# Feed-forward down projection over both streams as seven products, weight sums on GpSimd, in a two-layer encoder trunk

## The chip, the cores and the metric

One core of a Trainium2 chip runs the whole program. The metric is device time in microseconds (us), the median of three runs. The engines are TensorE (PE, with its weight loads PEld), VectorE (DVE), ScalarE (ACT), GpSimd (POOL) and SyncE (SP, which issues the loads).

## What is computed

Two streams of 512 tokens, width 1024, go through two layers with shared weights, and a final norm. The part at issue is the gated feed-forward of each layer, here from the reference:

```
h = _rmsnorm(x, norm_ffn)
gate, up = jnp.split(h @ ffn_w_up, 2, axis=-1)
gate = _dwconv3(gate, ffn_conv)
x = x + (jax.nn.gelu(gate) * up) @ ffn_w_down
```

`ffn_w_up` is 1024 x 5632 and `ffn_w_down` 2816 x 1024. Ahead of it stands a mixer (retention heads, a long convolution, pooling) with input and output projections, behind it a gate by a per-layer embedding.

## The kernel before

Activations lie transposed: 128 channels on the partitions, 512 tokens of one stream along the free axis. A width of 1024 is eight such tiles, the inner width of 2816 is 22.

**Three matmuls for one.** Each float32 operand is split into two float16 parts (`split`, L173): ACT writes the high part, DVE the rest. A product of two tiles is then three float16 matmuls of 128x128 by 512 columns: high by high, high by low, low by high.

**Weights.** SP loads raw float32 tiles (128x1024, `wraw`, four buffers) in the order of the list `TILES`; ACT and DVE split them into `wspl` tiles (nine buffers). The functions `plan_weights` and `prep` (L186, L217) cut this into pieces and issue them ahead of use, up to 21 us by a table of estimated step times (`step_time`, L115) and as far as the nine buffers allow.

**Up projection.** The first three of 22 pairs of a gate tile and an up tile are made for each stream by itself (`f.hn`, `fg`, `fu`). For the other 19 the two streams are taken together: the weight's two columns (gate, up), its two halves of K, and the two streams form a 2x2 by 2x2 product that needs seven products instead of eight (Strassen in Winograd's form). Such a pair is called a *unit* here. It needs sums of activations (`ffn_sums`, L1010, once per layer) and four sums of weights per unit (`piece_pair`, L273, on DVE before), which overwrite the raw tiles. The seven products run in three PSUM banks X, Y, Z, in the order X, Y, Z, X, Y, X, X (`ffn_joint`, L1038; `product`, L1096): the later ones accumulate onto what lies there, so each bank must be read between two of them. The results are read as `r1`, `r5`, `r2` (ACT copies) and by sums on DVE; then come the convolution (`conv3`, L556), the gelu, and `gated` (L1003), which multiplies by the up half and splits the result into an `at` tile for the down projection.

**Down projection.** The 22 `at` tiles of a stream are used in four parts (`PARTS`, L31): 6, 6, 5 and 5 of them. After the last unit of a part come its eight output tiles (`d0_0` to `d0_7` and so on), each for stream 0 and then stream 1 (`down`, L1034, with `mm3`, L302): for part 0 that is 6 x 3 matmuls each, and DVE adds the bank onto the residual tile `x`. The last part belongs to the streams' own threads (`main_thread`, L828).

**Order.** The list `STEPS` (`tile_order`, L87) fixes the order of these steps on PE. Within a layer it puts the first products of the next unit between the last two of a unit:

```
            last = steps.pop(cut)
            steps[cut:cut] = [seven[0], last, seven[1], seven[2]]
            steps += seven[3:]
```

So PE's order in the middle of the stage is: product 5 of unit j, product 0 of unit j+1, product 6 of unit j, products 1, 2, 3, 4, 5 of unit j+1. PE and SP keep the written order; DVE, ACT and POOL are put in order at build time by the tile framework, each then runs its queue strictly in that order.

## Time and profile before

| | |
|---|---|
| median of 3 runs | 2510.44 us (2508.78 to 2511.34) |
| the profiled execution: its time, its span | 2508.9 us, 2507.1 us |
| busy: PE, PEld | 2431.4 us (97%), 1191.8 us (48%), 12240 matmuls and as many loads |
| busy: DVE, ACT, POOL | 1639.4 us (65%), 985.7 us (39%), 368.3 us (15%) |
| stage of the joint units and down parts 0 to 2 | about 622 to 1141 us (layer 0), 1808 to 2327 us (layer 1) |

Busy times of PE overlap from one matmul to the next, since their ends are modelled; the start-to-start time is what a matmul costs. The same holds for DVE, more weakly: an instruction shown as 0.69 us is followed by the next one after 0.60 us. Rows of the trace name the line of the helper that records an instruction (L155 `act`, L158 `stt`, L161 `tt`), so they are told apart by their tiles.

### The profile page before, as it was taken

What the parts mean: (1) busy time and instruction counts of PE and PEld (TensorE: products, weight loads), DVE (VectorE), ACT (ScalarE), POOL (GpSimd) and SP (SyncE); (2) the same over time, 40 slices, a digit from 0 to 9 for tenths busy, and PEclk for the clock granted to TensorE, in tenths of its full rate; (3) what the DMA queues carried; (4) which work ended last, traced back from release to release, by engine and by line L of the source; (5) the groups of instructions that cost most, each with busy time, mean ns of one, the idle gap of its engine ahead of it and who ended that gap; (6) DMA issues with size and microseconds to landing.
All of it is one profiled execution on the core that took longest, in us unless ns stands there. A gap on an engine that the chain in (4) does not pass through costs nothing.

```text
span 2507.1 us, 30755 instructions
## 1 busy us (share of the span) xinstructions
PE 2431.4 (97%) x12240; PEld 1191.8 (48%) x12240; DVE 1639.4 (65%) x2530; ACT 985.7 (39%) x1567; POOL 368.3 (15%) x294
## 2 busy tenths in 40 slices
PE   5999989999999999999999999999999999999997
PEld 3544654444444444444456555544444444444443
DVE  6984886868737557475575686555964755757545
ACT  5543334345515325243533343333541532524441
POOL 3213343123000000000121223511300000000011
PEclk9999999999999999999999999999999999999998
DMA  6122020340201201112232111031021120212201
GB/s 221 64 82 75 25 69 18 116 133 34 82 34 62 73 34 59 51 68 87 69 121 89 65 48 52 28 112 64 34 68 34 64 72 34 68 43 76 84 1 67
DMA packets 63927, 168.05 MB, mean 67 GB/s; under 512 B 7526, under 2 KB 13670, under 8 KB 63784
## 3 DMA queue, kind: packets, MB, share of 16 engines
q1 hardware_dynamic: 57880, 155.87, 18.4%
q10 hardware_dynamic: 5904, 10.23, 1.1%
q8 instruction: 95, 1.56, 0.3%
q14 instruction: 48, 0.39, 0.1%
HBM read 151.65 MB, written 14.42 MB: 66 GB/s over the span
## 4 chain that ended last, share of the span: by engine, by line
PE 75%; DVE 4%; POOL 1%; issue 1%; ACT 1%; ACTq 0%; POOLq 0%; DVEq 0%
PE fx L1100 16%; PE fy L1100 8%; PE d L311 6%; PE d L309 6%; PE d L310 6%; PE fz L1100 4%; PE s L309 2%; PE s L311 2%; PE s L310 2%; PE o L310 2%; PE o L311 2%; PE o L309 2%; PE fu L309 1%; PE fu L311 1%; PE fu L310 1%
## 5 line engine op out<-in xcount | busy, mean ns | idle before, releaser
L155 ACT ACTIVATE wspl<-wraw 128x512 f16<-128x512 f32 (+3 forms) x426 | 309.9, 744 | 483.3 <-PE d L311 273.8
L1100 PEld LDWEIGHTS <-wspl 128*128 128x128 f16 x3192 | 312.3, 98 | 379.2 <-issue 2.8
L158 DVE SCALAR_TENSOR_TENSOR wspl<-wraw,wspl 128x512 f16<-128x512 f32 (+3 forms) x420 | 346.1, 837 | 110.9 <-ACT wspl L155 109.0
L309 PEld LDWEIGHTS <-wspl 128*128 128x128 f16 x2112 | 208.9, 99 | 250.4 <-issue 8.9
L311 PEld LDWEIGHTS <-wspl 128*128 128x128 f16 x2112 | 207.2, 98 | 252.4 <-issue 4.7
L310 PEld LDWEIGHTS <-wspl 128*128 128x128 f16 x2112 | 207.2, 98 | 252.2 <-issue 11.6
L1100 PE MATMUL fx<-hs,wspl 128*128 128x512 f16 x1368 | 313.9, 379 | 2.2 <-DVE r L161 2.2
L309 PE MATMUL d<-at,wspl 128*128 128x512 f16 x704 | 266.8, 379 | 0.0
L310 PE MATMUL d<-at,wspl 128*128 128x512 f16 x704 | 266.8, 379 | 0.0
L311 PE MATMUL d<-at,wspl 128*128 128x512 f16 x704 | 266.8, 379 | 0.0
L158 DVE SCALAR_TENSOR_TENSOR x<-d,x 128x512 f32<-128x512 f32 x128 | 88.5, 691 | 254.2 <-PE d L311 253.9
L161 POOL TENSOR_TENSOR y<-t,mhalf 128x4 f32<-128x4 f32 x30 | 36.3, 1211 | 1416.5 <-DVE t L165 1407.2
L158 DVE SCALAR_TENSOR_TENSOR conv<-r,scaled,conv 128x511 f32<-128x511 f32 x152 | 113.7, 748 | 44.3 <-ACT conv L155 42.6
L161 DVE TENSOR_TENSOR wraw<-wraw 128x512 f32<-128x512 f32 x152 | 104.3, 686 | 1.9
L1100 PE MATMUL fx<-h,wspl 128*128 128x512 f16 x456 | 104.6, 379 | 0.0
L1100 PE MATMUL fy<-h,wspl 128*128 128x512 f16 x456 | 104.6, 379 | 0.0
L1100 PE MATMUL fy<-hs,wspl 128*128 128x512 f16 x456 | 104.6, 379 | 0.0
L1100 PE MATMUL fz<-h,wspl 128*128 128x512 f16 x456 | 104.6, 379 | 0.0
L161 DVE TENSOR_TENSOR acc<-acc,sq 128x512 f32<-128x512 f32 x84 | 64.0, 766 | 51.0 <-ACT sq L155 49.7
L155 ACT ACTIVATE sq<-x 128x512 f32<-128x512 f32 x80 | 49.6, 624 | 121.4 <-DVE x L158 53.3
L311 PE MATMUL s<-xs,wspl 128*128 128x512 f16 x256 | 97.0, 379 | 0.0
L310 PE MATMUL s<-xs,wspl 128*128 128x512 f16 x256 | 97.0, 379 | 0.0
(236 smaller groups left out, 4417.9 us busy)
## 6 DMA issues: line engine op xcount, KB each, us to landing
wraw<-in_w SPq DMA_DIRECT2D x172, 512.0 KB, 3.5
wraw<-in_w SPq DMA_DIRECT2D x32, 384.0 KB, 3.3
wraw<-in_w SPq DMA_DIRECT2D x32, 320.0 KB, 3.0
x<-in_x SPq DMA_DIRECT2D x32, 256.0 KB, 4.1
dec<-ddec SPq DMA_DIRECT2D x16, 448.0 KB, 4.0
xsp<-x ACTq DMA_DIRECT2D x16, 256.0 KB, 2.1
x<-xsp SPq DMA_DIRECT2D x16, 256.0 KB, 3.8
out_y<-out SPq DMA_DIRECT2D x16, 256.0 KB, 2.2
```

The costliest lines, as they stand in the source:

```text
L155: return self.nc.scalar.activation(out=out, in_=in_, func=func, **k)
L158: return self.nc.vector.scalar_tensor_tensor(out=out, in0=in0, scalar=scalar, in1=in1, op0=op0, op1=op1)
L161: return (eng or self.nc.vector).tensor_tensor(out=out, in0=in0, in1=in1, op=op)
L309: self.nc.tensor.matmul(out, wv[:, 0, kb, :], x[:, 0], start=first, stop=False)
L310: self.nc.tensor.matmul(out, wv[:, 0, kb, :], x[:, 1], start=False, stop=False)
L311: self.nc.tensor.matmul(out, wv[:, 1, kb, :], x[:, 0], start=False, stop=last)
L1100: mm = lambda a, b, start=False, stop=False: self.nc.tensor.matmul(out, a, b, start=start, stop=stop, skip_group_check=not first)
```

## The change

- `PARTS` becomes 6, 6, 6 and 4 tiles, and the first three parts (`JOINT = 3`) are done for both streams together: two output tiles, the two members of each pair of `at` tiles, and the two streams form the 2x2 by 2x2 product, with seven products of 3 x 3 matmuls per pair of output tiles. The steps are `e{part}_{pair}.{0..6}`, in banks X, Y, Z as before, and DVE adds each of the seven results onto a residual tile.
- `gated` no longer only splits: for each pair of `at` tiles it makes four sums of activations on DVE and splits seven tiles instead of four.
- The weight tiles of two outputs are regrouped on the host (`pack`) into `ea`, `eb`, and go through `piece_pair` as the gate and up tiles do.
- In `piece_pair` the four weight sums move from DVE to POOL, and the seven splits of 512 columns become four: 1024, 512, 1024, 1024 (768, 384, 768, 768 for the down weights).
- The pool of general tiles grows from 64 to 70, and the scratch area for dynamic DMAs is set to 2048.

```diff
-PARTS = [(0, 6), (6, 12), (12, 17), (17, 22)]
+PARTS = [(0, 6), (6, 12), (12, 18), (18, 22)]
+JOINT = 3
...
-            if j == b - 1:
+            if j == b - 1 and t < JOINT:
+                tiles += [f"e{x}{t}_{i}" for i in range(NB // 2) for x in "ab"]
+
+                for i in range(NB // 2 + 1):
+                    now, old = ([f"e{t}_{k}.{q}" for q in range(7)] for k in (i, i - 1))
+                    if i == 0:
+                        steps += now[:5]
+                    elif i < NB // 2:
+                        steps += [now[0], old[5], now[1], now[2], old[6], now[3], now[4]]
+                    else:
+                        steps += old[5:]
+            elif j == b - 1:
...
-        self.gp = pool("gen", 64)
+        self.gp = pool("gen", 70)
...
-                    self.pieces += [(self.piece_pair, l, j, k) for k in range(7)]
-                wants.append((self.piece_pair, l, j, (0, 2, 3, 4, 5, 6, 6)[int(q)]))
+                    self.pieces += [(self.piece_pair, l, j, k) for k in range(4)]
+                wants.append((self.piece_pair, l, j, (0, 2, 2, 3, 3, 3, 3)[int(q)]))
...
     def piece_pair(self, l, j, k):
 
-        g, u = (self.rawt[l, n + j[1:]] for n in ("fg", "fu"))
-        a11, a12, a21, a22 = g[:, 0:512], g[:, 512:1024], u[:, 0:512], u[:, 512:1024]
-        if k in (0, 1, 3, 5):
-            self.wt[l, j, k] = self.wtile(l, f"{j}.{(1, 6, 3, 5)[(0, 1, 3, 5).index(k)]}")
-        t, half, q, src = ((0, 0, 0, a11), (1, 0, 6, a22), (0, 1, 1, a22), (3, 0, 2, a12), (3, 1, 3, a11),
-                           (5, 0, 4, a12), (5, 1, 5, a21))[k]
+        names, gq = self.raw_names(j), self.nc.gpsimd
+        g, u = (self.rawt[l, n] for n in names)
+        n = self.width(names[0]) // 2
+        a11, a12, a21, a22 = g[:, 0:n], g[:, n:2 * n], u[:, 0:n], u[:, n:2 * n]
         if k == 2:
-            self.tt(a22, a21, a22, ALU.add)
-            self.tt(a21, a11, a21, ALU.subtract)
-        elif k == 4:
-            self.tt(a11, a22, a11, ALU.subtract)
-        elif k == 5:
-            self.tt(a12, a12, a11, ALU.subtract)
-        w = self.wt[l, j, t][:, :, half * 512:half * 512 + 512]
-        self.split(w[:, 0], w[:, 1], src, WS)
-        self.wt[l, f"{j}.{q}"] = w
-        if k == 6:
+            self.tt(a22, a21, a22, ALU.add, gq)
+            self.tt(a21, a11, a21, ALU.subtract, gq)
+        elif k == 3:
+            self.tt(a11, a22, a11, ALU.subtract, gq)
+            self.tt(a12, a12, a11, ALU.subtract, gq)
+        src, qs = ((g, (0, 2)), (a22, (6,)), (u, (5, 1)), (g, (3, 4)))[k]
+        w, c = self.wtile(l, f"{j}.{(2, 6, 5, 4)[k]}"), len(qs) * n
+        self.split(w[:, 0, 0:c], w[:, 1, 0:c], src[:, 0:c], WS)
...
     def gated(self, f, s, c, up):
 
         self.stt(c, up, FFS / WS, c, ALU.mult, ALU.mult)
-        at = self.g([128, 2, T], F16, name="at")
-        self.split(at[:, 0], at[:, 1], c)
-        f.acts[s].append(at)
+
+        def part(t):
+            at = self.g([128, 2, T], F16, name="at")
+            self.split(at[:, 0], at[:, 1], t)
+            return at
+
+        j = f.count[s]
+        f.count[s] += 1
+        if j >= PARTS[JOINT][0]:
+            f.acts[s].append(part(c))
+            return
+        e, k = j // 2, j % 2
+        wide = f.wide.setdefault(e, {})
+        wide[s, k] = c
+        right = lambda q, t: f.right[q].__setitem__(e, part(t))
+        if (s, k) != (1, 0):
+            right({(0, 0): 0, (0, 1): 2, (1, 1): 4}[s, k], c)
+
+        if "t1" not in wide and (0, 0) in wide and (1, 0) in wide:
+            wide["t1"] = wide[0, 0]
+            self.tt(wide[0, 0], wide[1, 0], wide[0, 0], ALU.subtract)
+            right(1, wide[0, 0])
+        if "t2" not in wide and "t1" in wide and (1, 1) in wide:
+            self.tt(wide[1, 0], wide[1, 1], wide[1, 0], ALU.subtract)
+            right(5, wide[1, 0])
+            wide["t2"] = wide[1, 1]
+            self.tt(wide[1, 1], wide[1, 1], wide[0, 0], ALU.subtract)
+            right(3, wide[1, 1])
+        if "t2" in wide and (0, 1) in wide:
+            self.tt(wide[0, 1], wide[0, 1], wide[1, 1], ALU.subtract)
+            right(6, wide[0, 1])
+            del f.wide[e]
...
+            if name[0] == "e":
+                t, i = int(j[1]), int(j[3])
+                xs = [f.right[q][e] for e in range(PARTS[t][0] // 2, PARTS[t][1] // 2)]
+                self.product(p, w, xs, q < 3)
+                s, m = ((0, 0), (1, 1), (0, 0), (1, 0), (1, 0), (1, 1), (0, 1))[q]
+                x = f.x[s][2 * i + m]
+                self.stt(x, p, 1.0 / (WS * FFS), x)
```

What it does to the queues is seen at three places. The first is DVE's queue over one joint unit in the middle of layer 0 (`r1<-fz` is the step behind the third product, `r2<-fy` behind the fifth, `r5<-fx` behind the sixth; `wspl` are weight splits of the next unit). Before:

```order
L161 TENSOR_TENSOR r1_6509<-fz_6555,r1_6509 128x512
L161 TENSOR_TENSOR wraw_6456<-wraw_6454,wraw_6456 128x512
L158 SCALAR_TENSOR_TENSOR wspl_6616<-wraw_6456,wspl_6616 128x512
L161 TENSOR_TENSOR wraw_6454<-wraw_6456,wraw_6454 128x512
L158 SCALAR_TENSOR_TENSOR conv_6569<-r1_6509,scaled0_185,conv_6569 128x511 x2
L158 SCALAR_TENSOR_TENSOR wspl_6674<-wraw_6454,wspl_6674 128x512 x2
L161 TENSOR_TENSOR wraw_6454<-wraw_6454 128x512
L161 TENSOR_TENSOR r2_6590<-fy_6537,r2_6590 128x512
L158 SCALAR_TENSOR_TENSOR conv_6611<-r2_6590,scaled0_185,conv_6611 128x511
L161 TENSOR_TENSOR r5_6550<-fx_6496,r5_6550 128x512
```

And of the change:

```order
L176 TENSOR_TENSOR r1_6527<-fz_6581,r1_6527 128x512
L173 SCALAR_TENSOR_TENSOR wspl_6675<-wraw_6453,wspl_6675 128x512
L173 SCALAR_TENSOR_TENSOR conv_6595<-r1_6527,scaled0_185,conv_6595 128x511 x2
L176 TENSOR_TENSOR r2_6612<-fy_6557,r2_6612 128x512
L173 SCALAR_TENSOR_TENSOR wspl_6680<-wraw_6453,wspl_6680 128x1024
L173 SCALAR_TENSOR_TENSOR conv_6627<-r2_6612,scaled0_185,conv_6627 128x511
L176 TENSOR_TENSOR r5_6570<-fx_6514,r5_6570 128x512
L173 SCALAR_TENSOR_TENSOR conv_6627<-r2_6612,scaled0_185,conv_6627 128x511
L173 SCALAR_TENSOR_TENSOR wspl_6720<-wraw_6451,wspl_6720 128x1024
L173 SCALAR_TENSOR_TENSOR conv_6627<-r5_6570,conv_6627 128x512
L176 TENSOR_TENSOR conv_6492<-conv_6627,conv_6492 128x512
L176 TENSOR_TENSOR at_6649<-conv_6627,at_6649 128x512
```

The weight sums (`wraw<-wraw`) are gone from DVE, a 1024-wide split that needs POOL's sums now stands between `r2` and `r5`, and sums and splits of activations (`conv<-conv,conv`, `at`) follow.

The second place is DVE's queue at the end of down part 0 of layer 0 in the change (`ey`, `ex` are banks of the last pair of output tiles; the last two rows with `ex_6352` belong to its products 5 and 6, which are neighbours on PE):

```order
L173 SCALAR_TENSOR_TENSOR x_4954<-ex_6352,x_4954 128x512
L173 SCALAR_TENSOR_TENSOR wspl_6413<-wraw_6257,wspl_6413 128x1024
L173 SCALAR_TENSOR_TENSOR x_4954<-ey_6373,x_4954 128x512
L173 SCALAR_TENSOR_TENSOR x_4999<-ex_6352,x_4999 128x512
L173 SCALAR_TENSOR_TENSOR wspl_6448<-wraw_6255,wspl_6448 128x1024
L173 SCALAR_TENSOR_TENSOR wspl_6497<-wraw_6348,wspl_6497 128x1024
L173 SCALAR_TENSOR_TENSOR x_4690<-ex_6352,x_4690 128x512
```

Before, each output tile had a bank of its own and no product there waited for a reading of its bank.

The third is POOL's queue ahead of the joint stage of layer 0 (`y` and `hn`, `h` belong to the norm and `ffn_sums`). Before:

```order
L161 TENSOR_TENSOR khat_4995<-khat_4995,bias_3258 128x512
L161 TENSOR_TENSOR y_5072<-t_5071,mhalf_87 128x4
L161 TENSOR_TENSOR hn_4896<-hn_5183,hn_4896 128x512
L161 TENSOR_TENSOR h_5185<-hn_5183,h_5185 128x512
L161 TENSOR_TENSOR hn_4906<-hn_5193,hn_4906 128x512
```

And of the change:

```order
L176 TENSOR_TENSOR y_5072<-t_5071,mhalf_87 128x4
L176 TENSOR_TENSOR wraw_5094<-wraw_5094 128x512
L176 TENSOR_TENSOR wraw_5094<-wraw_5035,wraw_5094 128x512
L176 TENSOR_TENSOR wraw_5035<-wraw_5094,wraw_5035 128x512
L176 TENSOR_TENSOR wraw_5035<-wraw_5035 128x512
L176 TENSOR_TENSOR hn_4896<-hn_5183,hn_4896 128x512
```

The four weight sums of the first unit stand ahead of the activation sums on POOL; those of the following units come behind them, four for each unit and each pair of output tiles.

## Rows read from the trace of the kernel before

**Rows 1.** The page: busy time by engine, and the granted clock in 40 slices.

```profile
PE 2431.4 (97%) x12240; PEld 1191.8 (48%) x12240; DVE 1639.4 (65%) x2530; ACT 985.7 (39%) x1567; POOL 368.3 (15%) x294
...
PEclk9999999999999999999999999999999999999998
```

**Rows 2.** Waits of PE in all: line, releaser, us in total, times, longest.

```profile
PE fx L1100 <- DVE r L161: 2.2, 2, 1.1
```

**Rows 3.** Busy time in two stretches: joint units, then down part 1.

```profile
core 0: us, PE busy (x) PEld busy (x) DVE busy (x) ACT busy (x) POOL busy (x), PEclk, DMA share, GB/s
770.00:850.00 80.00, 80.00 (x373) 36.28 (x371) 60.22 (x91) 40.60 (x68) 0.00 (x0) 1.00 0.20 66
856.00:918.00 62.00, 62.00 (x289) 28.14 (x288) 22.13 (x32) 7.86 (x12) 0.00 (x0) 1.00 0.13 43
```

**Rows 4.** The chain that ended last, in order of time: start, us, what.

```profile
798.93 2.59 PE fz L1100 x12
801.52 2.59 PE fx L1100 x12
804.12 2.59 PE fy L1100 x12
806.71 7.77 PE fx L1100 x36
```

**Rows 5.** Groups on DVE by form: busy us, mean ns, then idle before.

```profile
L158 DVE SCALAR_TENSOR_TENSOR wspl<-wraw,wspl 128x512 f16<-128x512 f32 x266 | 177.1, 686 | 36.6 <-ACT wspl L155 36.4
L158 DVE SCALAR_TENSOR_TENSOR conv<-r,scaled,conv 128x511 f32<-128x511 f32 x152 | 113.7, 748 | 44.3 <-ACT conv L155 42.6
L158 DVE SCALAR_TENSOR_TENSOR wspl<-wraw,wspl 128x1024 f16<-128x1024 f32 x90 | 112.0, 1245 | 36.5 <-ACT wspl L155 35.7
L161 DVE TENSOR_TENSOR wraw<-wraw 128x512 f32<-128x512 f32 x152 | 104.3, 686 | 1.9
L158 DVE SCALAR_TENSOR_TENSOR x<-d,x 128x512 f32<-128x512 f32 x128 | 88.5, 691 | 254.2 <-PE d L311 253.9
L161 DVE TENSOR_TENSOR at<-conv,at 128x512 f16<-128x512 f32 x88 | 64.9, 737 | 29.5 <-ACT at L155 28.5
L158 DVE SCALAR_TENSOR_TENSOR wspl<-wraw,wspl 128x768 f16<-128x768 f32 x32 | 30.6, 957 | 18.8 <-ACT wspl L155 18.8
```

**Rows 6.** DVE in order of time in a joint unit (800 to 850).

```profile
802.17 0.68 DVE L161 TENSOR_TENSOR wraw<-wraw 128x512 f32<-128x512 f32 x1
802.77 0.69 DVE L158 SCALAR_TENSOR_TENSOR wspl<-wraw,wspl 128x512 f16<-128x512 f32 x1
...
809.37 0.68 DVE L161 TENSOR_TENSOR r<-fx,r 128x512 f32<-128x512 f32 x1
```

**Rows 7.** DVE in order of time, 1735 to 1812, while POOL is busy.

```profile
1769.83 1.39 DVE L158 SCALAR_TENSOR_TENSOR hn<-x,vec,rb 128x512 f32<-128x512 f32 x2
...
1777.55 1.75 DVE L161 TENSOR_TENSOR at<-conv,at 128x512 f16<-128x512 f32 x1
```

**Rows 8.** POOL in order of time, from several stretches.

```profile
1341.25 1.26 POOL L161 TENSOR_TENSOR rt<-rt,sw 128x512 f32<-128x512 f32 x1
...
1399.67 2.13 POOL L161 TENSOR_TENSOR rt<-rt,sw 128x512 f32<-128x512 f32 x1
...
1459.25 0.72 POOL L161 TENSOR_TENSOR t<-t,t 128x256 f32<-128x256 f32 x1 [25.36 <-DVE t L161]
...
1763.90 1.27 POOL L161 TENSOR_TENSOR hn<-hn 128x512 f32<-128x512 f32 x1 [10.16 <-DVE hn L158]
...
1775.37 5.07 POOL L161 TENSOR_TENSOR hn<-hn 128x512 f32<-128x512 f32 x3
```

**Rows 9.** Groups on ACT by form.

```profile
L155 ACT ACTIVATE at<-conv 128x512 f16<-128x512 f32 x88 | 55.2, 628 | 53.7 <-DVE conv L158 51.7
L155 ACT ACTIVATE wspl<-wraw 128x1024 f16<-128x1024 f32 x96 | 100.8, 1051 | 84.0 <-PE o L311 34.0 <-PE d L311 28.7 <-PE s L311 5.0
```

**Rows 10.** PE in order of time, end of the joint stage of layer 0.

```profile
1138.06 2.75 PE L1100 MATMUL fx<-hs,wspl 128*128 128x512 f16 x12
1141.93 2.75 PE L1100 MATMUL fx<-hs,wspl 128*128 128x512 f16 x12 [1.12 <-DVE r L161]
...
1147.11 0.38 PE L309 MATMUL d<-at,wspl 128*128 128x512 f16 x1
```

**Rows 11.** DVE in order of time, the same stretch.

```profile
1141.20 0.69 DVE L161 TENSOR_TENSOR r<-fx,r 128x512 f32<-128x512 f32 x1
...
1146.11 0.69 DVE L161 TENSOR_TENSOR at<-conv,at 128x512 f16<-128x512 f32 x1 [0.69 <-ACT at L155]
```

More of the change, by code (lines that the diff above doesn't have):

```diff
@@ L115, in step_time @@
 def step_time(name):
+    if name[0] == "e":
+        a, b = PARTS[int(name[1])]
+        return 0.3225 * (b - a)
     if "." in name:
@@ L199, in plan_weights @@
                 if q == "0":
-                    self.raws += [(l, "fg" + j[1:]), (l, "fu" + j[1:])]
-                    self.pieces += [(self.piece_pair, l, j, k) for k in range(7)]
-                wants.append((self.piece_pair, l, j, (0, 2, 3, 4, 5, 6, 6)[int(q)]))
+                    self.raws += [(l, r) for r in self.raw_names(j)]
+                    self.pieces += [(self.piece_pair, l, j, k) for k in range(4)]
+                wants.append((self.piece_pair, l, j, (0, 2, 2, 3, 3, 3, 3)[int(q)]))
             self.at.append(clock)
@@ L246, in width, with raw_names @@
     def width(self, name):
-        if name[0] != "d":
+        if name[0] not in "de":
             return 1024
-        a, b = PARTS[int(name[1])]
+        a, b = PARTS[int(name[1 if name[0] == "d" else 2])]
         return (b - a) * 128
+    def raw_names(self, j):
+        return ("fg" + j[1:], "fu" + j[1:]) if j[0] == "f" else ("ea" + j[1:], "eb" + j[1:])
     def load_raws(self, ahead=RBUFS):
@@ L273, in piece_pair @@
     def piece_pair(self, l, j, k):
[L275 to L291 removed]
+        names, gq = self.raw_names(j), self.nc.gpsimd
+        g, u = (self.rawt[l, n] for n in names)
+        n = self.width(names[0]) // 2
+        a11, a12, a21, a22 = g[:, 0:n], g[:, n:2 * n], u[:, 0:n], u[:, n:2 * n]
+        if k == 2:
+            self.tt(a22, a21, a22, ALU.add, gq)
[6 more added lines that the diff above has]
+        self.split(w[:, 0, 0:c], w[:, 1, 0:c], src[:, 0:c], WS)
+        for i, q in enumerate(qs):
+            self.wt[l, f"{j}.{q}"] = w[:, :, i * n:(i + 1) * n]
+        if k == 3:
             self.freed += 2
[L293 removed]
+            for n in names:
+                del self.rawt[l, n]
     def weight(self, l, name, *ss):
@@ L1048, in ffn_joint @@
         for name in STEPS[first:end]:
-            if name[0] == "d":
-                t, m = int(name[1]), int(name[3:])
-                for s in range(2):
-                    if m == 0:
-                        f.down[s], f.acts[s] = f.acts[s], f.acts[s][PARTS[t][1] - PARTS[t][0]:]
-                    self.weight(l, name, 0, 1)
-                    self.down(l, t, m, s, f.down[s][:PARTS[t][1] - PARTS[t][0]], f.x[s])
-                    if m == NB - 1:
-                        f.down[s] = None
-                yield 1.29 * (PARTS[t][1] - PARTS[t][0]), 0.0
-                continue
-            j, q = name[1:].split(".")
-            j, q = int(j), int(q)
+            j, q = name.split(".")
+            q = int(q)
             w = self.weight(l, name, 0, 1)
@@ L1064, in ffn_joint @@
             if q in (0, 1, 2):
-                st["XYZ"[q]] = self.bank(name="f" + "xyz"[q])
+                st["XYZ"[q]] = self.bank(name=name[0] + "xyz"[q])
             p = st["XYZXYXX"[q]]
+            if name[0] == "e":
+                t, i = int(j[1]), int(j[3])
[4 more added lines that the diff above has]
+                self.stt(x, p, 1.0 / (WS * FFS), x)
+                if q in (2, 4):
+                    del st["Z" if q == 2 else "Y"]
+                if q == 6:
+                    del state[j]
+                if i == NB // 2 - 1:
+                    for e in range(PARTS[t][0] // 2, PARTS[t][1] // 2):
+                        del f.right[q][e]
+                st = p = xs = x = None
+                yield step_time(name), 0.0
+                continue
+            key, j = j, int(j[1:])
             self.product(p, w, right[q], q < 3)
@@ L1091, in ffn_joint @@
                 self.gated(f, 0, st.pop("c0"), p)
-                del state[j]
+                del state[key]
             st = p = None
@@ L1096, in product @@
     def product(self, out, w, xs, first):
-        for kb in range(4):
+        n = len(xs)
+        for kb in range(n):
             wh, wl = (w[:, i, kb * 128:(kb + 1) * 128] for i in range(2))
@@ L1188, in __init__ @@
         self.h, self.x, self.hn, self.sums = [None, None], [None, None], [[], []], None
-        self.acts, self.down, self.done = [[], []], [None, None], Event()
+        self.acts, self.done = [[], []], Event()
+        self.count, self.wide, self.right = [0, 0], {}, [{} for _ in range(7)]
         self.over = Event()
@@ L1337, in pack @@
             for t, (k0, k1) in enumerate(PARTS):
-                put(l, f"d{t}_{m}", a["ffn_w_down"][l][k0 * 128:k1 * 128, c])
+                wd = a["ffn_w_down"][l][k0 * 128:k1 * 128, c]
+                if t < JOINT:
+                    wd = wd.reshape(-1, 2, 128, 128).transpose(1, 0, 2, 3).reshape(-1, 128)
+                    put(l, f"e{'ab'[m % 2]}{t}_{m // 2}", wd)
+                else:
+                    put(l, f"d{t}_{m}", wd)
         for j in range(NPAIR):
```

5 lines of the change are left out of this document (2 added, 3 removed).

## The prediction

> **What bounds the kernel now.** I read the page first: PE is busy 97% of the span, and the granted clock is at its upper level, 2.4 GHz, but for the last slice [rows 1]. Since PE's busy time is modelled, the next view is what PE waited for. In the joint stages there are just two such waits, one in each layer, 2.2 us together [rows 2]. The chain that ended last then shows PE following itself through the units: twelve matmuls per product, 2.59 us, so 0.2158 us for one, and a unit of seven products takes 18.13 us [rows 4]. The stretches say the same of the down parts, where PE is full and DVE is busy 22 of 62 us; in the units it is busy 60 of 80 [rows 3]. So TensorE bounds this stage, a matmul that goes is worth 0.2158 us, and the question is whether DVE, the next busiest, still keeps up.
>
> **Part 1: fewer matmuls.** Before, the down projection is 22 tiles x 3 matmuls x 8 outputs x 2 streams = 1056 per layer. Now it is 3 parts x 4 pairs x 7 products x 9 = 756, and 4 x 3 x 8 x 2 = 192 in the last part: 948. That is 108 fewer per layer, 216 in all: **-46.6 us**. The loads of weights shrink alike, and raw bytes stay the same.
>
> **Part 2: the end of each joint part.** Within a part two other products stand between those that share a bank; but behind the last pair, products 5 and 6 are neighbours on PE and both use X. PE must wait there until DVE has read X. The same happens today once per layer, where the last unit ends: the product began at 1138.06 and lasted 2.59 us, DVE's read began at 1141.20 behind other work, and PE went on at 1141.93 [rows 10, 11]. That is a gap of 1.12 us; from the read's start to PE's it is 0.73. In the new queue nothing that waits stands right ahead of this read, so I take 0.1 + 0.73, about 0.8, for each of the six parts: **+4.8 us** (4.4 if the read starts at once, 6.7 if it is as late as in the row).
>
> **Part 3: four tiles in the last part.** Its first product needs the newest `at` tile last. Today that is at the 13th matmul, 1147.11 [rows 10], and DVE ends its split at 1146.80 [rows 11], just in time. With four tiles it is the 10th, 0.65 us earlier, so PE waits about 0.4 us per layer: **+0.8 us** (0 to 1.3).
>
> **Part 4: DVE in a unit.** DVE instructions of 512 columns follow each other in 0.60 us, though shown as 0.69 [rows 6]; taking the same 0.09 off the rows, a split of 1024 costs 1.15, of 768 0.87, a step of the convolution 0.66 [rows 5]; for 384, which no row has, I take 0.45 (half of 768, and at most the 0.60 of 512). Four weight sums leave per unit, seven splits become four of the same columns; two activation sums and one and a half more `at` splits come in. Counted along the new queue, a unit that completes a pair of `at` tiles holds 13 short instructions, 4 convolution steps and 3 wide splits: 7.8 + 2.6 + 3.5 = 13.9 us. The other holds 10 short ones: 12.1 us. Both lie under 18.1.
>
> **Part 5: POOL against DVE.** Four sums per unit now run on POOL. Alone one takes 1.26 us [rows 8]. While POOL is busy, a DVE instruction with one operand in PSUM is not slowed (1.39 us for two), but one with both in SBUF takes 1.75 instead of 0.69 [rows 7]: it waits 1.06 us for POOL. The reverse is seen too: POOL takes 1.69 us each against short DVE work (three in 5.07), and 2.13 behind a split of 1024 [rows 8]. Their SBUF work is done in turn. Per unit POOL then holds 4 x 1.06 = 4.2 us; if all of it stopped DVE, two units would need 13.9 + 12.1 + 8.5 = 34.5 of 36.3 us. So on average it fits, with little to spare.
>
> **Part 6: the read that PE needs.** The step that counts is `r5`: it reads X behind product 5, and product 6 writes X after one other product. Take the end of product 2 as zero. Product 5 ends at 7.8, and PE needs the read done by 10.4 [rows 4]; today it starts at 809.37, 0.07 us after its product ends at 809.30 [rows 4, 6], and is done 1.8 us ahead of need. In the new queue a split of 1024 that needs two of POOL's sums stands ahead of it. Laid out from the rows: the 512 split is done at 1.3; two POOL sums and two convolution steps take turns, 2 x (1.06 + 0.66) = 3.4, until 4.7; ACT does the gelu and then the high half, 0.63 + 1.05 [rows 9], until 6.4; POOL's other two sums end near 7.1; the split ends at 8.3, a convolution step at 8.9, and `r5` at 9.6. That leaves 0.8 us; in every other unit a left-over split comes first, and 0.2 us is left. I take a small loss, 0.1 us for each of the 38 units: **+4 us** (0, if the layout holds, to 40, if each is late by one POOL instruction).
>
> **The rest costs nothing.** Down parts: a pair of output tiles takes 63 x 0.2158 = 13.6 us of PE, DVE needs 7 x 0.60 + 3 x 0.87 + 0.45 = 7.3, and POOL four sums of 384, by rows between 0.72 (256) and 1.27 (512), say 1.0 each; if that cover went, DVE would have 2.3 us left. The four weight sums ahead of the joint stage stand in front of `hn` on POOL, where POOL idles 10.2 us before it in layer 1 and needs 5.1 [rows 8]. ACT gains three splits per pair of tiles, 0.63 us each [rows 9], and loses short ones; in the units it was busy 41 of 80 us [rows 3]. Raw loads keep their order on SP, and the scratch area and pool size alter no instruction of the queues; DMA was busy a fifth of the time there [rows 3].
>
> **Sum.** 2508.9 (profiled execution) - 46.6 + 4.8 + 0.8 + 4 = 2471.9. The median shown is 1.5 above that execution: **2473 us**.
>
> **Rivals.** *(a) The port makes r5 late in most units.* If POOL gets in once more than laid out, r5 is late by 1.06 - 0.8 = 0.3 us in one unit and 0.9 in the next, on average 0.6: 38 x 0.6 = 23 us instead of 4, hence 2492. For it: the margins are thinner than one POOL instruction. Against it: PSUM readers pass freely, and a lighter unit follows each full one. The Trainium skill warns of this step (Perfetto Trace Analysis, "Optimizing Scalar/DVE Operations"): the two engines share a port into SBUF, so moving operations between them might not help. The trace agrees that they take turns (1.75 against 0.69 us); by that rule the 4.2 us per unit come back as waits, which is this case. The same section advises breaking instructions up where DVE, unsaturated, holds up another engine, which speaks against the wider splits: unsplit, 0.55 us of the 1.15 would not stand ahead of `r5`.
>
> *(b) Slower: DVE's head waits for POOL.* If each of the sums falls behind a wide split, as in the 2.13 us row, two of them end at 1.3 + 4.3 = 5.6, the high half at 7.3, the other two sums at 9.8, the split at 11.0, and `r5` at 12.3, 1.9 us too late in each unit: 38 x 1.9 = 72, and 2473 - 4 + 72 = 2541. It decides once a unit loses more than 41/38 = 1.1 us. Against it: only three wide splits stand in a unit for four sums, and two of the three wait for the sums themselves.
>
> *(c) The matmuls go, but no time.* If the stage were held by something with the pace of the units, such as raw loads, nothing would change: 2508. The waits speak against it: the two short ones on DVE are all that PE has in these stages [rows 2].
>
> **How the numbers follow.** Forecast 0.66; (a) 0.25, with anything between it and no gain in it; (b) 0.06; (c) 0.03. The range takes the best ends of the bounds, 2508.9 - 46.6 + 4.4 + 0 + 1.5 = 2468, less 2 for what the order shifts elsewhere, and reaches up to (a): 2466 to 2492; it leaves out (b), (c) and the upper part of (a). Two runs of this kernel can be told apart at about 0.2%, 5 us. Faster: 0.66 + 0.25 = 0.91; no change: 0.03; slower: 0.06.
>
> **What would show it.** 12024 matmuls; PE waits on `ex <- DVE x`, six of about 0.8 us; the units still 18.1 us apart. DVE's splits and sums inside a unit should show means well above 0.69 us, its PSUM readers not; POOL's weight sums 1.3 to 2.1 us. If PE shows waits on `fx <- DVE r` in most units, it is (a); if these exceed 1 us each, (b). I would be wrong if the chain leaves PE for DVE and POOL inside the units.

## The result, and the profile after

| | before | after |
|---|---|---|
| median (lowest to highest) | 2510.69 us (2508.78 to 2511.34, 4 runs) | 2483.3 us (2481.28 to 2487.51, 4 runs) |
| profiled execution: time, span | 2508.9, 2507.1 us | 2481.28, 2479.6 us |
| matmuls | 12240 | 12024 |

The ratio is 0.9894, 95% interval [0.9877, 0.9911]: faster by 27.4 us. Forecast were 2473 us, 37 us less than before; the time lies inside the range of 2466 to 2492.

The page of after, busy time of PE, the granted clock and the chain by engine, answers to [rows 1]:

```profile
PE 2387.3 (96%) x12024; PEld 1170.0 (47%) x12024; DVE 1769.6 (71%) x2510; ACT 1033.7 (42%) x1555; POOL 702.9 (28%) x542
...
PEclk9999999999999999999999999999999999999998
...
PE 41%; issue 23%; POOL 12%; DVE 5%; ACT 1%; POOLq 0%; ACTq 0%; DVEq 0%
```

The 216 matmuls are gone, POOL's busy time has nearly doubled, and the chain now leaves PE for POOL. That alone does not make POOL the bound. The chain stays on POOL's queue from one group of sums to the next, and most of what it counts there is time in which POOL does nothing:

```profile
788.84 10.57 issue
799.44 1.27 POOL wraw L176
```

What the stage lost is read from PE. The two stretches of [rows 3], in the same columns, show that PE is no longer full in either:

```profile
770.00:850.00 80.00, 78.63 (x364) 35.51 (x363) 69.19 (x86) 42.33 (x65) 23.80 (x16) 1.00 0.17 56
856.00:918.00 62.00, 61.22 (x285) 27.67 (x283) 39.38 (x51) 17.12 (x21) 22.19 (x19) 1.00 0.21 65
```

In 80 us of units PE loses 1.4, in the 62 us that hold most of down part 1 it loses 0.8. What it waits for, from the view of waits of after (us in total, times, longest); before there was only the line of [rows 2]:

```profile
PE fx L1156 <- DVE r L176: 8.7, 11, 1.2
PE fx L1156 <- ACT r L170: 6.4, 2, 3.8
...
PE ex L1156 <- DVE x L173: 4.7, 6, 0.8
```

These are three different places.

**The ends of the parts** (`ex <- DVE x`, six times 0.78). PE and DVE of after in order of time, end of part 0 in layer 0:

```profile
740.63 2.10 PE L1156 MATMUL ex<-at,wspl 128*128 128x512 f16 x9 [0.78 <-DVE x L173]
...
739.89 0.69 DVE L173 SCALAR_TENSOR_TENSOR x<-ex,x 128x512 f32<-128x512 f32 x1 [0.69 <-PE ex L1156]
```

DVE reads X at 739.89, as soon as product 5 has ended, and PE goes on 0.74 us later. This is part 2 as laid out.

**The read `r5` in the light units** (a full unit is one that completes a pair of `at` tiles, a light one the unit between two such; up to the end of part 2 a layer has seven light ones). Eight of the eleven waits are of 0.7 us, two in the units of part 1 and two in those of part 2 of each layer, 37.1 us apart, with a full unit between them. One of 0.77 at 661.34 is in a light unit too; two of 1.19 stand at the ends of the two stages. So nine of 14 light units are late; in time are the first light one in part 1 and in part 2 of each layer, and that of part 0 in layer 1. Four engines of after in order of time, around the wait at 790.05:

```profile
779.46 0.63 ACT L170 ACTIVATE at<-conv 128x512 f16<-128x512 f32 x1 [2.03 <-DVE conv L176]
779.99 0.58 ACT L170 ACTIVATE r<-fy 128x512 f32<-128x512 f32 x1
780.47 0.62 ACT L170 ACTIVATE wspl<-wraw 128x512 f16<-128x512 f32 x1
...
781.12 0.69 DVE L173 SCALAR_TENSOR_TENSOR wspl<-wraw,wspl 128x512 f16<-128x512 f32 x1 [0.31 <-ACT wspl L170]
...
781.89 6.95 POOL L176 TENSOR_TENSOR wraw<-wraw 128x512 f32<-128x512 f32 x4 [13.58 <-DVE wspl L173]
...
787.64 1.75 DVE L173 SCALAR_TENSOR_TENSOR conv<-r,scaled,conv 128x511 f32<-128x511 f32 x1
789.31 0.68 DVE L176 TENSOR_TENSOR r<-fx,r 128x512 f32<-128x512 f32 x1
...
790.05 2.75 PE L1156 MATMUL fx<-hs,wspl 128*128 128x512 f16 x12 [0.69 <-DVE r L176]
```

It is the queue of part 6. A left-over `at` split stands first on ACT; the 512 split that POOL waits for is done at 781.8; POOL's four sums follow at 1.74 us each until 788.84; and the convolution step right ahead of `r5` lasts 1.75 us, because the fourth sum runs beside it. In the full units the sums are done before that (799.44 to 805.41 in the next one), and `r5` is in time.

**The first unit of each layer** (`fx <- ACT r`). ACT and PE of after, and the busy times and the granted clock (behind the five busy times) of five microseconds of layer 1:

```profile
630.75 0.63 ACT L170 ACTIVATE at<-conv 128x512 f16<-128x512 f32 x1 [1.77 <-DVE conv L176]
631.29 0.58 ACT L170 ACTIVATE r<-fx 128x512 f32<-128x512 f32 x1
...
631.92 2.75 PE L1156 MATMUL fx<-hs,wspl 128*128 128x512 f16 x12 [3.76 <-ACT r L170]
...
1804.37 4.41 PE L1156 MATMUL fx<-hs,wspl 128*128 128x512 f16 x12 [2.65 <-ACT r L170]
1808.62 2.75 PE L1156 MATMUL fy<-h,wspl 128*128 128x512 f16 x12
```

```profile
1804.00:1809.00 5.00, 4.63 (x14) 1.77 (x14) 4.15 (x5) 2.12 (x5) 2.79 (x2) 0.66 0.00 0
```

The copy `r1` (the trace leaves the numbers out: `r<-fx`), which PE's product 3 needs, stands on ACT behind an `at` split of the three plain pairs, and that one waits for an activation sum on DVE. In layer 1 the granted clock is 0.66 right behind the wait, between its two levels of 1.2 and 2.4 GHz, and the product takes 4.25 us to the next instead of 2.59: 1.7 us more.

The view of waits counts from the modelled end of a matmul, and a product of twelve is shown as 2.75 us where the next one follows after 2.59; so each wait in the view cost 0.16 us more than it says. The stage from start to start, from the first joint product to the first matmul of the last part, was in layers 0 and 1:

| | matmuls | length | less 0.2158 us each |
|---|---|---|---|
| before | 2412, 2412 | 521.87, 521.87 us | 1.36, 1.36 us |
| after | 2352, 2352 | 520.05, 519.70 us | 12.5, 12.1 us |

So the stages lost 21.9 us more than before: 8.4 in the first units (the clock's 1.7 among it), 7.9 at `r5` and 5.6 at the ends of the parts. With 25.9 for their 120 matmuls they are 4.0 us shorter. The rest of the program is 23.5 us shorter (1463.4 to 1439.8); the 96 matmuls of the last part are 20.7 of that. The other 2.8 us lie where the change alters little, and are not explained; in the kernels of the experiments with the joint down projection this rest is 1438 to 1446 us (1456 in e5). Together that is -4.0 - 23.5 = -27.5, as measured (2479.6 - 2507.1).

At last the groups of after, DVE and POOL by form, that answer to [rows 5] (busy us, mean ns):

```profile
L173 DVE SCALAR_TENSOR_TENSOR conv<-r,scaled,conv 128x511 f32<-128x511 f32 x152 | 165.1, 1086 | 7.9 <-ACT conv L170 4.7
L173 DVE SCALAR_TENSOR_TENSOR x<-ex,x 128x512 f32<-128x512 f32 x96 | 66.2, 690 | 63.1 <-PE ex L1156 62.1
...
L176 POOL TENSOR_TENSOR wraw<-wraw 128x512 f32<-128x512 f32 x152 | 227.6, 1497 | 404.7 <-DVE wspl L173 394.8 <-DVE rr L180 1.0
```

The convolution steps, both operands in SBUF, went from 748 to 1086 ns; the reads of PSUM stayed at 690.

### The profile page after: what moved, and what is told of

It is laid out like the page before. It is cut to its first block, busy times and chain, and to the rows that moved or that the text cites. A ratio compares the mean times of both kernels' runs of the same rounds, so it can differ in the third digit from the quotient of the medians.

```text
span 2479.6 us, 30852 instructions
## 1 busy us (share of the span) xinstructions
PE 2387.3 (96%) x12024; PEld 1170.0 (47%) x12024; DVE 1769.6 (71%) x2510; ACT 1033.7 (42%) x1555; POOL 702.9 (28%) x542
## 4 chain that ended last, share of the span: by engine, by line
PE 41%; issue 23%; POOL 12%; DVE 5%; ACT 1%; POOLq 0%; ACTq 0%; DVEq 0%
POOL wraw L176 10%; PE fx L1156 4%; PE ex L1156 3%; PE fy L1156 2%; PE s L328 2%; PE s L330 2%; PE s L329 2%; PE o L329 2%; PE o L330 2%; PE o L328 2%; PE ey L1156 1%; PE d L329 1%; PE d L328 1%; PE d L330 1%; PE fz L1156 1%
## 5 line engine op out<-in xcount | busy, mean ns | idle before, releaser
L176 POOL TENSOR_TENSOR wraw<-wraw 128x512 f32<-128x512 f32 (+1 forms) x248 | 331.2, 1335 | 684.2 <-DVE wspl L173 668.6
L170 ACT ACTIVATE wspl<-wraw 128x1024 f16<-128x1024 f32 (+2 forms) x360 | 326.9, 911 | 427.4 <-POOL wraw L176 102.4
L173 DVE SCALAR_TENSOR_TENSOR wspl<-wraw,wspl 128x1024 f16<-128x1024 f32 (+2 forms) x354 | 391.3, 1107 | 85.2 <-ACT wspl L170 84.7
L1156 PE MATMUL ex<-at,wspl 128*128 128x512 f16 x864 | 196.3, 379 | 4.7 <-DVE x L173 4.7
L173 DVE SCALAR_TENSOR_TENSOR conv<-r,scaled,conv 128x511 f32<-128x511 f32 x152 | 165.1, 1086 | 7.9 <-ACT conv L170 4.7
L170 ACT ACTIVATE at<-conv 128x512 f16<-128x512 f32 x142 | 88.8, 626 | 107.2 <-DVE conv L176 68.8
L176 DVE TENSOR_TENSOR at<-conv,at 128x512 f16<-128x512 f32 x142 | 103.4, 737 | 25.5 <-ACT at L170 23.6
L173 DVE SCALAR_TENSOR_TENSOR x<-ex,x 128x512 f32<-128x512 f32 x96 | 66.2, 690 | 63.1 <-PE ex L1156 62.1
L170 ACT ACTIVATE conv<-conv 128x512 f32<-128x512 f32 x88 | 55.4, 630 | 120.4 <-DVE conv L173 120.1
L1156 PE MATMUL ey<-at,wspl 128*128 128x512 f16 x432 | 101.1, 379 | 0.0
```

What stands on the lines that cost most here:

```text
L170: return self.nc.scalar.activation(out=out, in_=in_, func=func, **k)
L173: return self.nc.vector.scalar_tensor_tensor(out=out, in0=in0, scalar=scalar, in1=in1, op0=op0, op1=op1)
L176: return (eng or self.nc.vector).tensor_tensor(out=out, in0=in0, in1=in1, op=op)
L1156: mm = lambda a, b, start=False, stop=False: self.nc.tensor.matmul(out, a, b, start=start, stop=stop, skip_group_check=not first)
```

## The experiments

Each ratio is to the kernel before, run on the same chip; its times there had a median of 2508.3 to 2509.9 us.

### The three waits, one by one

**e1_defer** holds back the sums and splits of the plain pairs' stream 1 (eleven steps in a layer) and issues them in the joint units. The third plain pair's difference thereby comes behind the sums of the first unit that should use it, so this kernel leaves that dependency out and sums other values; number and sizes of the instructions are the same.

```diff
...
+        late = s == 1 and j < PLAIN
+        todo = f.late if late else []
...
+        if j >= PLAIN:
+            n = 2 if j > PLAIN or s == 0 else 3
+            for step in f.late[:n]:
+                step()
```

> The activation sums and splits of the plain pairs of stream 1 (11 instructions per layer) are held back and done two at a time inside the first joint units. Theory A, the loss sits at a few places of their own: the first unit's wait of 3.8 and 2.7 us on ACT's copy goes, and with it the 1.7 us at the lower clock behind it in layer 1, so about 8 us less than the change, 2475 us; the waits on r5 and on ex stay as they are. Theory B, DVE is short of time all through the stage, by the port it shares with POOL: the work moved into the units makes as much waiting there, r5 is late in units 3 to 5 by a microsecond or more, and the time stays at 2483 us.

Measured: 2482.65 us, ratio 0.9896 [0.9879, 0.9912], the same as after. PE's waits:

```profile
PE fx L1168 <- DVE r L176: 9.5, 11, 1.6
PE fy L1168 <- ACT r L170: 4.9, 2, 2.5
```

The wait in the first unit is gone, and in the second unit stands one of 2.5 us in each layer and, in layer 0, one of 1.6 on `r5`. The work found no room there. Whether there is none at all, or only none while POOL's sums run, stayed open until e11 and e12.

**e2_gap** puts the next unit's product 3 between products 5 and 6 of a part's last pair.

```diff
-            steps += seven[3:]
+            if steps[-1][0] == "e":
+                steps[-1:] = [seven[3], steps[-1]] + seven[4:]
+            else:
+                steps += seven[3:]
```

> The next unit's product 3 is put between products 5 and 6 of the last pair of output tiles of each joint part. Theory A: the six waits of 0.78 us on ex go and nothing takes their place, 4.7 us less than the change, 2479 us. Theory B: the wait turns up again in the units behind, the time stays at 2483 us.

Measured: 2477.97 us, ratio 0.9877 [0.9862, 0.9891], 5.3 us less than after. In the view of waits nothing is left on `ex`:

```profile
PE fx L1159 <- DVE r L179: 8.0, 10, 1.2
PE fx L1159 <- ACT r L173: 6.5, 2, 3.8
```

So part 2's cost was real and a matter of order alone. The intervals of after and e2 overlap; that the time fell is read from the stages, 1035.0 us together against 1039.7 in after, though the clock fell behind the first unit's wait in both layers here. With the sums on DVE the same edit is clear in the time as well (e7 and e10 below).

**e3_far** puts two products instead of one between products 5 and 6 of a unit, which gives `r5` 2.59 us more.

```diff
-            steps[cut:cut] = [seven[0], last, seven[1], seven[2]]
+            steps[cut:cut] = [seven[0], seven[1], last, seven[2]]
```

> In the units two products instead of one stand between product 5 and product 6, so that the reading of r5 has 5.2 instead of 2.6 us. Theory A: the nine waits of 0.7 us on r5 inside the units go, 6.5 us less than the change, 2477 us; the waits in the first unit and on ex stay. Theory B: DVE falls behind further and PE waits at the next reading, 2483 us.

Measured: 2490.91 us, ratio 0.9928 [0.9913, 0.9942], 7.6 us more than after: a miss. The waits, and ACT in order of time:

```profile
PE fx L1156 <- ACT r L170: 13.3, 10, 3.8
PE fx L1156 <- DVE r L176: 5.2, 10, 1.2
```

```profile
784.85 0.63 ACT L170 ACTIVATE at<-conv 128x512 f16<-128x512 f32 x1 [2.06 <-DVE conv L176]
...
785.99 0.57 ACT L170 ACTIVATE r<-fx 128x512 f32<-128x512 f32 x1
```

The waits for `r5` shrink to 0.35 us, but do not go. The `at` split moved back with product 6, and `r1` now stands behind it in ACT's queue: eight new waits of 0.85. The stages are 4.5 us longer than after's together (1044.3 against 1039.7); the rest of the 7.6 lies outside of them and is not accounted for. A later due time for one read is not a margin when the queue in front of it moves too.

**e4_nosum** leaves the weight sums out (the four `self.tt` in `piece_pair` are removed; the splits take the raw tiles as they are).

> The weight sums are left out altogether (the split weights are then those of the raw tiles). Theory A: without POOL in the port and without waiting for its results r5 is in time, the nine waits of 0.7 us go; the ex waits stay at 0.78 us; the first unit's wait on ACT shrinks at most by half, since the plain pairs' sums are still there: 6.5 to 10 us less than the change, 2473 to 2477 us. Theory B: every wait of PE in the stage goes but the ex ones, 15 us less, 2468 us.

Measured: 2473.04 us, ratio 0.9858 [0.9843, 0.9872], 10.3 us less than after.

```profile
PE ex L1150 <- DVE x L173: 6.4, 6, 1.1
PE fx L1150 <- ACT r L170: 3.3, 2, 2.2
PE fx L1150 <- DVE r L176: 2.4, 2, 1.2
```

Only the two ends of stage are left of the `r5` waits: the sums on POOL caused all the others, and half of the first unit's wait.

### The way in which POOL's sums cost time

**e5_wk** gives the 512 split its own three buffers.

```diff
...
-        w, c = self.wtile(l, f"{j}.{(2, 6, 5, 4)[k]}"), len(qs) * n
+        c = len(qs) * n
+        w = (self.wk.tile([128, 2, 512], F16, tag="wk", name="wk") if k == 1 else
+             self.wtile(l, f"{j}.{(2, 6, 5, 4)[k]}"))
```

> The 512 wide split of every unit (and the 384 one of every pair of output tiles) gets a small pool of its own, three buffers, so that it no longer waits for one of the nine weight buffers to come free; nothing else is altered. Theory A (order): in every other unit POOL's sums start late, because this split, on which they wait, stands behind a left-over activation split and behind a weight buffer; the fourth sum then falls on the convolution step right ahead of r5. With the split earlier, the sums end earlier, the waits of PE on fx <- DVE r of about 0.7 us in every other unit go, and the time falls by about 6.5 us to 2477. Theory B (port alone): POOL needs the port to SBUF as long as before, whenever it starts, and some instruction ahead of r5 pays for it: the waits stay at about 0.7 us, and the time stays at 2483 within 2 us.

Measured: 2527.59 us, ratio 1.0073 [1.0058, 1.0088], 44 us more than after and slower than before. Both theories missed it. The waits, and POOL in order of time ahead of the stage:

```profile
PE fx L1161 <- ACT r L173: 30.7, 22, 6.0
...
PE fg L334 <- POOL h L179: 10.1, 3, 4.7
```

```profile
567.32 9.48 POOL L179 TENSOR_TENSOR wraw<-wraw 128x512 f32<-128x512 f32 x6 [1.02 <-DVE rr L183]
...
583.96 3.40 POOL L179 TENSOR_TENSOR wraw<-wraw 128x512 f32<-128x512 f32 x2
587.33 1.28 POOL L179 TENSOR_TENSOR hn<-hn 128x512 f32<-128x512 f32 x1
```

Freed from the nine buffers, the sums of two units run ahead of the stage: two of them right in front of `hn` in the queue that also makes `h`, for which PE's `fg` waits. In the units they start beside the splits and sums of activations, and most of PE's waits are on ACT's copies `r`. The build puts the other splits in another order, too (the copy for which PE waits 1.51 us at 798.84 stands behind two wide weight splits in a row on ACT), so this run does not tell the two apart.

**e6_aside** lets POOL do sums of the same size into a tile that nobody reads, and the splits take the raw tiles as they are. (The spare tile takes the place of one of the 70 general ones.)

```diff
...
+        if k in (2, 3):
+            o = self.spare[:, 0:n]
+            self.tt(o, a21, a22, ALU.add, gq)
+            self.tt(o, a11, a21, ALU.subtract, gq)
```

> POOL does as many sums of the same size, but into a tile that nobody reads, so no split waits for a sum; the weights are used without their sums, which leaves that part of the computation out. POOL's use of the port stays, the waiting for its results goes. Theory A (what costs is that DVE's and ACT's split of 1024 stand in line behind the sums): the waits on fx <- DVE r in the units go, as they did when the sums were left out, and the time is 2474 to 2477. Theory B (what costs is the port): DVE instructions still last 1.75 us instead of 0.69 beside a sum, r5 is late by some tenths of a microsecond in every other unit, and the time stays at 2480 to 2484.

Measured: 2503.53 us, ratio 0.9977 [0.9966, 0.9987], 20 us more than after: outside both theories, and the clearest look at the port. Of it 14.0 us are in the two stages. Waits, then POOL, DVE and ACT in order of time:

```profile
PE fy L1155 <- ACT r L170: 14.5, 10, 2.9
```

```profile
779.85 7.31 POOL L176 TENSOR_TENSOR spare<-wraw 128x512 f32<-128x512 f32 x4 [11.87 <-DMA wraw<-in_w]
...
780.93 3.43 DVE L176 TENSOR_TENSOR at<-conv,at 128x512 f16<-128x512 f32 x2
784.39 1.64 DVE L176 TENSOR_TENSOR conv<-conv 128x512 f32<-128x512 f32 x1
...
786.07 0.63 ACT L170 ACTIVATE at<-conv 128x512 f16<-128x512 f32 x1 [5.12 <-DVE conv L176]
786.60 0.58 ACT L170 ACTIVATE r<-fy 128x512 f32<-128x512 f32 x1
```

No split waits for these sums, and the `r5` waits in the units are gone; but the sums start when the raw tile lands, beside the splits and sums of activations. Two of these splits (`at<-conv,at`) take 3.43 us; in after, at 777.41, the two take 1.28, and DVE's and ACT's instructions around them stand in the same order. ACT's `at` split waits for DVE's sum behind them, the copy `r<-fy` stands behind it, and PE waits 1.85 at 787.23. So sums whose results nobody waits for cost time through the port, and how much depends on which work they fall beside. In after, the wait for the 512 split kept them away from these splits.

### The parts of the change alone

**e7_dvesum** puts the weight sums back on DVE, with wide splits kept.

```diff
-        names, gq = self.raw_names(j), self.nc.gpsimd
+        names, gq = self.raw_names(j), None
```

> The weight sums go back to DVE; wide splits and the joint down projection stay. DVE then holds 13.9 + 4 x 0.6 = 16.3 us of the 18.1 of a unit that completes a pair of activation tiles, 14.5 of the other, and none of its instructions is held up by POOL. Theory A (POOL's delay, not DVE's load, made r5 late): the waits of 0.7 us go, the wait in the first joint unit of a layer grows from 3.2 us to 4 or 5, and the time is 2477 to 2483. Theory B (DVE's load decides, so that moving the sums to POOL was needed): r5 is late by 0.5 us or more in the units that complete a pair, too, and the time is above 2490.

Measured: 2478.49 us, ratio 0.9884 [0.9869, 0.9899], and as Theory A said, no `r5` wait in any unit, the two of 1.19 at the ends of stage alone:

```profile
PE ex L1156 <- DVE x L173: 6.7, 6, 1.1
PE fx L1156 <- ACT r L170: 6.5, 2, 3.9
...
PE fx L1156 <- DVE r L176: 2.4, 2, 1.2
```

The growth of the first unit's wait did not come. DVE carried the sums; the move to POOL was not needed to keep up.

**e8_solo** is the kernel before, with its own down projection, but with the sums on POOL and the wide splits.

> The kernel before with the weight sums on POOL and the wide splits, but with its own down projection: three matmuls per tile and stream, no sums of activations. Theory A (the sums on POOL cost PE something only where left-over activation splits and sums stand in the queue as well): no wait in the units, 2508 to 2512. Theory B (the sums on POOL by themselves make r5 late): waits on fx <- DVE r in most of the 38 units, 0.2 to 0.7 us each, 2516 or more. Rival C (the move is a gain by itself, since DVE is freed): under 2505.

Measured: 2508.52 us, ratio 0.9997 [0.9988, 1.0006]. No wait in the units, although DVE's convolution steps are slowed as in after:

```profile
L158 DVE SCALAR_TENSOR_TENSOR conv<-r,scaled,conv 128x511 f32<-128x511 f32 x152 | 155.0, 1020 | 4.6 <-ACT conv L155 0.4
```

An instruction that takes longer costs nothing where the read behind it is still in time; here no left-over split or activation sum of the joint down projection stands ahead.

**e9_joint** is the joint down projection with sums on DVE and seven narrow splits.

```diff
-        names, gq = self.raw_names(j), self.nc.gpsimd
+        names, gq = self.raw_names(j), None
...
-        self.split(w[:, 0, 0:c], w[:, 1, 0:c], src[:, 0:c], WS)
+        for i in sorted(range(len(qs)), key=lambda i: k != 0 and qs[i] not in (1, 3)):
+            self.split(w[:, 0, i * n:i * n + n], w[:, 1, i * n:i * n + n], src[:, i * n:i * n + n], WS)
```

> The joint down projection alone: the weight sums stand on DVE and the weights of a unit are split in seven pieces, as in the kernel before. Theory A (the matmuls saved are the whole gain, the other two parts of the change bring nothing, since DVE has the time for sums and short splits): no waits in the units, six waits of about 1 us at the ends of the parts and the one in the first unit of each layer, 2476 to 2482. Theory B (without the other two parts DVE is too short of time): waits on fx <- DVE r or <- ACT r in the units that complete a pair of activation tiles, 2488 or more.

Measured: 2480.7 us, ratio 0.9885 [0.9869, 0.9902]. These three runs take the change apart: the joint product gives all of the gain (e9), the other two parts by themselves none that can be measured (e8). Whether the sums on POOL take something back, as PE's waits say (8.7 against 2.4 us for `r5`), the intervals of after and e7 are too near to tell; the pairs below do.

### Put together

**e10_gapd** is e7 with e2's gap, **e11_gapd3** also holds back the plain pairs' eleven steps, with the third pair's ahead, and puts them one behind each product from product 4 of the first unit on (two behind the first), and **e12_gappool3** is e11 with the sums on POOL.

```diff
...
+        if late:
+            f.late = todo + f.late if j == PLAIN - 1 else f.late + todo
+            return
...
+            if f.late and (j > PLAIN or q >= 4):
+                f.late.pop(0)()
+                if j == PLAIN and q == 4:
+                    f.late.pop(0)()
             yield 2.58, 0.0
```

> The weight sums on DVE as in e7_dvesum, and the first unit's product behind the last pair of a part as in e2_gap. If the two costs are separate, both gains add up: no waits in the units, none at the ends of the parts, the one in the first unit of each layer left (3 to 4 us and the slower clock behind it), 2472 to 2475. Rival: with the gap filled, the read behind it moves onto DVE's sums, and r of the next unit comes late by 0.3 us or more six times: 2476 to 2479.

> As e10_gapd; besides, the sums and splits of the plain pairs' activations of stream 1 (11 steps in each layer) are held back and put one behind each product, two in the first joint unit and the rest in the next two. Theory A (DVE is short of time only at the start of the stage, and the units that follow have 1.8 us and more to give): the wait of PE in the first unit falls from 3 to 4 us to under 1, the clock stays at its upper level behind it, and 2466 to 2470. Theory B (the units that follow have nothing to give at the places that count, as e1_defer showed for a coarser shift): new waits on r of 1 us and more in the second and third unit, 2472 or more.

> e11_gapd3 with the weight sums back on POOL, nothing else altered: the pair tells what the move of the sums to POOL is worth by itself, under the best order found. Theory A (on POOL the sums make DVE late in the light units, on DVE they don't): waits on fx <- DVE r of about 0.7 us in every other unit come back, 16 to 18 of them in the two layers at most, and the time is 2470 to 2477, 6 to 12 us above e11_gapd3. Theory B (the place of the sums makes no difference): 2464 within 3 us, and no waits in the units.

| sums on POOL | | stages | sums on DVE | | stages |
|---|---|---|---|---|---|
| after | 0.9894 [0.9877, 0.9911] | 1039.7 us | e7 | 0.9884 [0.9869, 0.9899] | 1036.6 us |
| + gap (e2) | 0.9877 [0.9862, 0.9891] | 1035.0 us | + gap (e10) | 0.9848 [0.9834, 0.9863] | 1028.2 us |
| + gap, spread steps (e12) | 0.9888 [0.9871, 0.9904] | 1033.4 us | + gap, spread steps (e11) | 0.9821 [0.9807, 0.9836] | 1019.9 us |

The stages are those of the two layers together, from start to start in the profiled execution.

e10 took 2470.53 us, e11 2464.38, e12 2479.85. e10 is as the theory of separate costs had it, and 1.5 us below its range. e11 is as its Theory A had it, 1.6 us below the range given; e12 is 15.5 us above e11, where its Theory A said 6 to 12, and above the range given; the stages alone differ by 13.4. PE's waits on `r5` in e11, then in e12:

```profile
PE fx L1172 <- DVE r L179: 2.8, 4, 1.2
```

```profile
PE fx L1172 <- DVE r L179: 13.5, 12, 2.8
```

With POOL's sums, the eight waits of 0.7 in the light units are back, and `r5` of the second unit, around which most of the moved steps stand, is 2.78 us late in each layer; without POOL's sums the same place waits 0.20. That answers what e1 left open: spread out, the eleven steps find room in the units, but not while POOL holds DVE up. e11 beats both kernels, the one before by 45.0 us (2509.41 in the same comparison) and the change by 18.9.

## Why the prediction was right, and where its sum was off

**The bound and part 1** held. PE bounds the stage, a matmul is worth 0.2158 us, and 216 of them are the whole gain: the last part and what follows it took 164.3 us in layer 0 before (1141.93 to 1306.26) and 154.1 after (1137.69 to 1291.77), 10.2 less, about 48 x 0.2158 = 10.4.

**Part 2** (+4.8) came to 5.6: from product 5 to product 6 it is 2.88 us instead of 1.94 (737.75 to 740.63), six times 0.94. That the read starts at once was taken rightly from the new queue, but hangs on the order: in e4, e7 and e9 it starts late. **Part 3** (+0.8) came to nothing: PE shows no wait where the last part begins.

**Part 4** held as far as it went: DVE has time in the units, and e7 shows that it would even have had it with the weight sums.

**Part 5 and part 6** (+4) had the mechanism and missed the size, 7.9. The price of one meeting, 1.06 us, was right, and so was the weak spot: the light unit. Its margin was laid out as +0.2 us and was -0.7. The layout counted a left-over split on DVE; it did not count that on ACT this split and the copy `r<-fy` stand ahead of the 512 split, which came 1.1 us later than laid out. In the full units the margin held, as laid out. A small loss in each of 38 units was the wrong shape as well: it was about 0.9 us (0.7 to 0.8 in the view) in nine light ones, and nothing in the full ones.

**The step that failed** is "the rest costs nothing". It costed the activation sums in a unit and forgot those of the three plain pairs, which stand at the start of the stage, where no unit covers them: 6.7 us of wait, and 1.7 at a lower clock. That these steps are the cause is shown by e1, e11 and e12, where they are moved and the first unit does not wait; that the weight sums have a share in it, by e4, where without them half of the wait is left (on DVE, in e7, they leave it at 6.5 us in the view, against 6.4). With the other terms' differences (+0.8 in part 2, -0.8 in part 3, +3.9 in parts 5 and 6) that makes 12.3 us; the profiled execution stood 2481.28 - 2471.9 = 9.4 above the sum. The gap between the two is for the most part the unexplained 2.8 us outside of the stages: that the sum was no further off is luck to this extent.

**The sign of being wrong.** The prediction would be wrong "if the chain leaves PE for DVE and POOL inside the units". The chain did leave PE for POOL, so by its words the sign came. But the chain of after holds mostly idle time of POOL there (10.57 of the 11.84 us of the two rows above), and the units of PE stand 18.1 us apart but for the late ones. The sign was badly chosen: the waits of PE tell what the stage lost, the chain's shares do not.

**Rival (a)** described the eight light units well: it had them 0.9 late, they waited 0.7. It did not become the case because the full units stayed in time, and five of the 14 light ones. The Trainium skill's page Perfetto Trace Analysis, section "Optimizing Scalar/DVE Operations", was cited for it: moving operations between two engines that share a port might not help. The runs agree: e8 gives nothing (0.9997), and e11 against e12 makes it a loss of 15.5 us. The section's other advice, to break instructions up, showed no effect with the sums on DVE, where `r5` is in time anyway: e9 with narrow splits and e7 with wide ones are alike. With the sums on POOL, where it might help, no run here tried it. **Rival (b)** did not occur. e5 is slower than before too, but by other waits: PE waits 30.7 us for ACT's copies there, and 3.9 for `r5`. **Rival (c)** fell with the result.

## What to carry to other kernels

Cost a new step in every stage in which it is issued, the first pass through a loop above all, where the work of the lead-in still stands in the queues. An engine that shares a port is no free place: count what its instructions run beside, since in these runs the same four sums per unit cost nothing (e8 against before), 7 us (e2 against e10), 15 (e12 against e11), or 20 more than in after (e6). Compare two kernels over the stage that the edit touches, from start to start, before the whole time is compared. When a wait in a queue is to be mended, look what was kept in place by it: a buffer that is freed lets work run ahead, and it may run into something worse.

## What the runs showed that was not expected

- Whether the granted clock falls behind PE's wait in the first unit is not settled by the wait's length: in after it stayed at 1.00 behind 3.76 us in layer 0 and was 0.66 in the five microseconds behind 2.65 us in layer 1; in e2 the product behind the wait took 4.27 us instead of 2.59 in both layers, behind 3.79 and 2.68 us; in e12 a wait of 2.78 us in the second unit left it at 1.00 in both layers. A fall costs 1.7 us on top of the wait in after and e2, and up to 2.5 in other kernels (e6 in layer 1, e7 in layer 0); in e11, with no wait at that place, neither layer shows it.
- One pool of three buffers, which adds no instruction, moved the time by 44 us (e5).
- The waits at the ends of the parts are longer without POOL's sums (1.06 to 1.11 us in e4, e7 and e9, 0.78 after). In these three traces a weight split stands right ahead of the read on DVE, and the read starts 0.3 to 0.4 us behind the product's end instead of at once; e4 in layer 0, where the product ends at 739.23:

```profile
738.41 1.22 DVE L173 SCALAR_TENSOR_TENSOR wspl<-wraw,wspl 128x1024 f16<-128x1024 f32 x1 [0.40 <-ACT wspl L170]
739.55 0.68 DVE L173 SCALAR_TENSOR_TENSOR x<-ex,x 128x512 f32<-128x512 f32 x1
```

No run moved that split.
